# Squares of x summed on VectorE for one product, positions loaded between x's pieces, and GpSimd taken out of MLA and RWKV

## The chip, the cores and the metric

The kernel runs on one core of a Trainium2 chip. The metric is the device time of one execution in microseconds (us). Before the change the median of 3 runs is 1454.68 us (1453.99 to 1456.4).

A core has engines with an instruction queue each, worked off in order: TensorE (PE, matrix products), VectorE (DVE), ScalarE (ACT), GpSimd (POOL) and SyncE (SP), which here only issues transfers. An instruction waits at the head of its queue until what it needs has been signalled; everything behind it on that engine waits too.

## The reference

Two transformer blocks work on 256 tokens of 1024 numbers, in float32. The parts that matter here:

```python
def rms_norm(x, g):
    xf = x.astype(jnp.float32)
    y = xf * lax.rsqrt(jnp.mean(xf * xf, axis=-1, keepdims=True) + EPS)
    return (y * g.astype(jnp.float32)).astype(x.dtype)

h = x                                              # first block
u = rms_norm(h, g_mix) @ w_in                      # then rope on q, k; attention, cross attention, MLP
...
p = rms_norm_2(x, g_mix) @ w_in                    # second block
y_a = mla_group(p[..., :MLA_COLS], positions, ...) # attention with q, k normed per head and rotated in part
y_b = rwkv7_group(p[..., MLA_COLS:], ...)          # p + (prev - p) * mu, then a recurrence in chunks of 64
x = x + jnp.concatenate([y_a, y_b], axis=-1) @ w_o
x = x + peer_ffn(rms_norm_2(x, g_ffn), w_pq, ...)  # top-k choice of experts
```

In `mla_group` scores are scaled by the norms of query and key before the softmax. In `rwkv7_group` the keys are scaled by `a` and by a decay, and the output is normed per head.

## The kernel before

Activations lie transposed, channels on the 128 partitions and the 256 tokens along the row. A weight slab (128x1024 float32) is loaded, ScalarE rounds it to a high part (`hi`, L330), VectorE subtracts to get the low part (`lo`, L332), and three products (high by high, high by low, low by high) give a result near float32: L351, L352 and L354 in `lin` matmuls. A 128x256 matmul of them starts 0.12 us after the one before. The results stand in four banks called `lin`.

The program is written as Python generators and loops, and a scheduler fixes the order of each engine's queue when the program is built, from its own estimate of the times. What is told here of order is thus a consequence of the code and not written in it.

The stages in time: 0 to 72 us the start (load x, its mean square, the tables of the rotation, first slabs); to 436 us the rest of the first block; to 660 us the second block's `w_in2`, MLA and RWKV, and the output product `w_o`; to 800 us the choice of experts; to the end the experts themselves.

**Start.** x comes in five pieces (L252). For each of its eight 128x256 parts, `sumsq` (L504) squares it, on ScalarE or (every second one) GpSimd, and a product with `ones` on TensorE (L513) adds it up in `lin_139`: eight products. `act_split` (L356) makes the high and low part of x (`xsh`, `xsl`, L364). `rsq` (L488) turns the sum into `rb`, the inverse root, with two refining steps on VectorE. `trig` (L562 on) makes sines and cosines of the positions, one table on VectorE and one on GpSimd. The first seven slabs go through the `lin` matmuls without the norm, and evacuating a bank multiplies by `rb` (L635).

**Block 2, 436 to 660 us.** `ev2` (L992) evacuates a part of `w_in2`: product with the norm into `pr`, difference to the token before on GpSimd (L1016), and back on VectorE (L1018). `lo_engines` with `LO2S = 'VVVVG'` sends every fifth low part to GpSimd. RWKV runs in two generators `r0` and `r1` of four heads each, MLA in a third one. In RWKV GpSimd multiplies `kk` and `kp` by the decay `Ls` (L1091, L1098) and scales by `ln_w` (L1194). In MLA, `rotate` (L1451) lets GpSimd multiply and add (L1455, L1456); `scale_keys` (L1371) calls `rsq` in its light form, with two products on GpSimd (L500); `scores` (L1381) takes the row maximum (L1390), scales it (L1391), and the exponential and its sum follow; L1399 scales the result `me` and TensorE transposes it (L1405). `outputs` (L1410) forms one pair of heads: `myo` on VectorE, then its high part `y2h` on ScalarE (L660).

The end of an RWKV generator, as far as it matters: TensorE adds the last products into `w` (L1292, L1298); ScalarE squares (L1309), VectorE multiplies (L1310), TensorE sums per head (L1315), ScalarE takes the inverse root (L490, L491), VectorE finishes (L1317, L1318), ScalarE takes the high part `y2h` (L1319) and VectorE the low part (L1320). `lo2` multiplies all eight parts of `y2` by `w_o`.

The residual h was written out ("spill") since its place is used for RWKV's matrices. It is read back in four transfers (L1540, in the order 0, 2, 1, 3), each of which waits for the last reader of the matrices in its place: transfer 0 for r0's first matrices, transfer 2 for the ones that L1298 of r0 reads, 1 and 3 for r1's. GpSimd multiplies each by `r4` (L1541).

Of the kernel before, what the change touches and what calls it, by code (L numbers as in the profile page):

```python
# [9 lines left out]
F32 = mybir.dt.float32  # L10
# [10 lines left out]
P = 128  # L21
# [39 lines left out]
LIGHT = True  # L61
# [5 lines left out]
LO2S = 'VVVVG'  # L67
# [148 lines left out]
def body(tc, A, out):  # L216
# [3 lines left out]
    with es:  # L220
# [28 lines left out]
        for j0, j1 in ((0, 1), (1, 2), (2, 4), (4, 6), (6, 8)):  # L249
            if j0 == X_W:  # L250
                ahead = [load(A["w_in_s"][FIRST[0]])]
            nc.sync.dma_start(xt[:, j0:j1], A["xT"][:, j0:j1])  # L252
            if j0 == 0:
                nc.sync.dma_start(pv, A["pv"])
        if X_W > 6:
            ahead = [load(A["w_in_s"][FIRST[0]])]
# [19 lines left out]
        cst = early.tile([P, CL["inv"][0] - CB], F32, name="cst")  # L276
        nc.sync.dma_start(ident, A["consts"][:, :P])
        pi = st.tile([P, 2, T], I32, name="posi")
        for j in range(2):
            nc.sync.dma_start(pi[:, j], bass.AP(tensor=A["pos"].tensor, offset=A["pos"].offset + j * T, ap=[[0, P], [1, T]]))  # L280
        inv = const.tile([P, 4], F32, name="inv")
        nc.sync.dma_start(inv, A["consts"][:, CL["inv"][0]:])
# [205 lines left out]
        def rsq(dst, ss, n, eps=EPS, newton=None, tag="n", light=False, am=None):  # L488
# [3 lines left out]
            if newton is not None or am is not None:  # L492
                if am is None:
                    am = newton.tile(list(dst.shape), F32, tag=tag + "a", name=nm("am"), bufs=1)
                if light:
                    S.activation(am, ss, AF.Identity, scale=-0.5 / n, bias=NEPS[:dst.shape[0]])
                else:
                    V.tensor_scalar(am, ss, -0.5 / n, -0.5 * eps, op0=OP.mult, op1=OP.add)
                for _ in range(2):
                    (G if light else V).tensor_tensor(am, am, dst, op=OP.mult)  # L500
                V.scalar_tensor_tensor(dst, am, 1.5, dst, op0=OP.add, op1=OP.mult)
            return ins
# [140 lines left out]
        for j, (g, f) in enumerate((("g_qn", 96.0 ** -0.5), ("g_kn", 1.0))):  # L643
            G.tensor_scalar(tabs[:, 2 * j], mc[:, 0], pvc(g), f, op0=OP.mult, op1=OP.mult)
            G.tensor_scalar(tabs[:, 1 + 2 * j], mc[:, 1], pvc(g), f, op0=OP.mult, op1=OP.mult)
# [345 lines left out]

        def ev2(nb, ps):  # L992
            if nb < 5:
                c = ml.tile([P, T], F32, tag="prd", name=nm("cq"))
                V.tensor_tensor(c, ps, r5, op=OP.mult)
                i, dst, g = (nb, cqp, "g_cq") if nb < 3 else (nb - 3, ckp, "g_ckv")
                act_split(dst, c, i, pvc(g, i))
                i = nb // 3
                ssk[i].add(c)
                if nb == 2:  # L1000

                    p_ = ssk[0].col()
                    for i in range(2):
                        V.tensor_scalar(ecol[:, 2 * i:2 * i + 2], p_[:, 0:2], EPS / 384, EPS * EPS, op0=OP.mult, op1=OP.add)
                    ssk[1] = SumSq(ml, 2)
                elif nb == 4:
                    rsq(rk2, ssk[1].ps(True)[:, :T], 256, newton=ml, tag="n96")
            elif nb == 5:
                V.tensor_tensor(kro[64:], ps[64:], r5[64:], op=OP.mult)
            else:  # L1010
                b = nb - 6
                pr = ml.tile([P, T + 1], F32, tag="pr", name=nm("pr"))
                G.memset(pr[:, 0:1], 0.0)
                V.tensor_tensor(pr[:, 1:], ps, r5, op=OP.mult)
# [32 lines left out]
        def rwkv(g):  # L1047
# [43 lines left out]
            G.tensor_tensor(kk, kk, Ls, op=OP.mult)  # L1091
# [6 lines left out]
            G.tensor_tensor(kp, kp, Ls, op=OP.mult)  # L1098
# [224 lines left out]
        def mla():  # L1323
# [103 lines left out]
            def project(j):  # L1427
# [19 lines left out]
                S.activation(kgu[0:64], ksq[0:64], AF.Copy, scale=pvc("g_kn")[0:64])  # L1447
# [3 lines left out]
            def rotate(qf, qg):  # L1451
# [3 lines left out]
                G.tensor_tensor(qg, qf, b2(tabs[:, 0]), op=OP.mult)  # L1455
                G.tensor_tensor(qg[rr], qg[rr], t2[rr], op=OP.add)  # L1456
# [24 lines left out]
        lo_engines[:] = [{"V": V, "G": G}[c] for c in LO2S]  # L1481
# [53 lines left out]
        RESE = G  # L1535
# [275 lines left out]
```

## Time and profile before

| | us |
|---|---|
| median of the runs | 1454.68 |
| profiled execution | 1457.07 |
| span of its trace | 1455.3 |
| TensorE busy | 1421.4 (98%) |
| VectorE busy | 1061.5 (73%) |
| ScalarE busy | 767.3 (53%) |
| GpSimd busy | 148.1 (10%) |

The shares are means over the whole span. The end is set where TensorE waits, and a table by stretch shows where that is: a wait of the bounding engine counts, and idle time of another one costs nothing. The clock column is the granted share of TensorE's full speed.

### The profile page before, as it was taken

What the parts mean: (1) busy time and instruction counts of PE and PEld (TensorE: products, weight loads), DVE (VectorE), ACT (ScalarE), POOL (GpSimd) and SP (SyncE); (2) the same over time, 40 slices, a digit from 0 to 9 for tenths busy, and PEclk for the clock granted to TensorE, in tenths of its full rate; (3) what the DMA queues carried; (4) which work ended last, traced back from release to release, by engine and by line L of the source; (5) the groups of instructions that cost most, each with busy time, mean ns of one, the idle gap of its engine ahead of it and who ended that gap; (6) DMA issues with size and microseconds to landing.
All of it is one profiled execution on the core that took longest, in us unless ns stands there. A gap on an engine that the chain in (4) does not pass through costs nothing.

```text
span 1455.3 us, 25592 instructions
## 1 busy us (share of the span) xinstructions
PE 1421.4 (98%) x9950; PEld 1287.5 (88%) x9950; DVE 1061.5 (73%) x1900; ACT 767.3 (53%) x1248; POOL 148.1 (10%) x159
## 2 busy tenths in 40 slices
PE   8999999999999988999999999999999999999998
PEld 7888999888898867899999999999998888888887
DVE  7876676886659988579999778788875555555554
ACT  6856655555557445554445444444445454454443
POOL 6500101000115443220000000000000000000000
PEclk9999999999999998999999999999999999999999
DMA  6543445566665411155555555555455555555554
GB/s 209 175 156 102 144 144 154 183 190 201 198 191 156 135 44 37 33 162 186 159 187 176 178 171 160 164 159 170 149 174 186 190 200 189 193 198 189 197 193 145
DMA packets 75914, 237.43 MB, mean 163 GB/s; under 512 B 14608, under 2 KB 17808, under 8 KB 75792
## 3 DMA queue, kind: packets, MB, share of 16 engines
q1 hardware_dynamic: 75792, 235.79, 50.9%
q8 instruction: 78, 1.28, 0.4%
q14 instruction: 44, 0.36, 0.1%
HBM read 233.27 MB, written 2.49 MB: 162 GB/s over the span
## 4 chain that ended last, share of the span: by engine, by line
PE 90%; DVE 6%; DMA 2%; ACT 1%; issue 1%; SPq 0%; POOL 0%; DVEq 0%; ACTq 0%
PE lin L354 17%; PE lin L351 13%; PE lin L352 13%; PE lin L348 8%; PE w L1788 8%; PE w L1787 8%; PE w L1791 8%; PE w L1709 2%; DVE lo L332 1%; PE lin L484 1%; PE lin L485 1%; PE lin L486 1%; DMA raw<-w_pq 1%; PE w L1623 0%; PE lin L513 0%
## 5 line engine op out<-in xcount | busy, mean ns | idle before, releaser
L332 DVE TENSOR_TENSOR lo<-raw,hi 128x1024 fp32r<-128x1024 f32 (+1 forms) x432 | 531.7, 1232 | 275.7 <-PE w L1788 97.2
L330 ACT ACTIVATE hi<-raw 128x1024 fp32r<-128x1024 f32 x437 | 459.0, 1050 | 467.8 <-DMA raw<-eu 99.2
L351 PE MATMUL lin<-hbh,hi 128*128 128x256 f32 x1024 | 253.0, 284 | 0.0
L352 PE MATMUL lin<-hbl,hi 128*128 128x256 f32 x1024 | 252.3, 284 | 0.0
L351 PEld LDWEIGHTS lin<-hbh,hi 128*128 128x128 f32 x1024 | 196.1, 192 | 0.1
L352 PEld LDWEIGHTS lin<-hbl,hi 128*128 128x128 f32 x1024 | 196.2, 192 | 0.0
L1788 PE MATMUL w<-lo,wh 128*128 128x512 f32 x504 | 155.6, 390 | 0.0
L1791 PE MATMUL w<-hi,wl 128*128 128x512 f32 x504 | 155.2, 389 | 0.0
L354 PE MATMUL lin<-hbh,lo 128*128 128x256 f32 x1024 | 145.0, 284 | 0.7 <-DVE lo L332 0.7
L1787 PE MATMUL w<-hi,wh 128*128 128x512 f32 x504 | 134.8, 389 | 0.0
L354 PEld LDWEIGHTS lin<-hbh,lo 128*128 128x128 f32 x1024 | 132.1, 192 | 1.1 <-DVE lo L332 1.1
L1791 PEld LDWEIGHTS w<-hi,wl 128*128 128x128 f32 x504 | 94.6, 188 | 19.7
L1787 PEld LDWEIGHTS w<-hi,wh 128*128 128x128 f32 x504 | 94.6, 188 | 19.6
L1788 PEld LDWEIGHTS w<-lo,wh 128*128 128x128 f32 x504 | 94.3, 188 | 19.5
L1770 ACT ACTIVATE wh<-GA 128x512 fp32r<-128x512 f32 x64 | 40.5, 634 | 73.2 <-PE w L1788 73.2
L530 POOL TENSOR_TENSOR sqa<-sqa,sq 128x256 f32<-128x256 f32 x37 | 34.7, 937 | 315.3 <-ACT sq L526 300.3
L348 PE MATMUL lin<-a,hi 128*128 128x512 f32 x256 | 64.8, 395 | 0.0
L348 PE MATMUL lin<-xs,hi 128*128 128x512 f32 x256 | 63.3, 392 | 0.0
L348 PEld LDWEIGHTS lin<-xs,hi 128*128 128x128 f32 x256 | 46.4, 189 | 8.5
L354 PE MATMUL lin<-xs,lo 128*128 128x256 f32 x384 | 53.8, 285 | 0.0
L348 PEld LDWEIGHTS lin<-a,hi 128*128 128x128 f32 x256 | 45.9, 188 | 8.5
L354 PEld LDWEIGHTS lin<-xs,lo 128*128 128x128 f32 x384 | 50.9, 191 | 2.2
(582 smaller groups left out, 2583.8 us busy)
## 6 DMA issues: line engine op xcount, KB each, us to landing
raw<-eu SPq DMA_DIRECT2D x128, 512.0 KB, 3.6
raw<-ev SPq DMA_DIRECT2D x128, 512.0 KB, 3.4
raw<-w_up SPq DMA_DIRECT2D x32, 512.0 KB, 3.6
raw<-w_down SPq DMA_DIRECT2D x32, 512.0 KB, 4.5
raw<-w_in SPq DMA_DIRECT2D x20, 512.0 KB, 3.6
raw<-w_in_s SPq DMA_DIRECT2D x16, 512.0 KB, 4.8
raw<-w_pq SPq DMA_DIRECT2D x16, 512.0 KB, 3.5
raw<-w_in_m SPq DMA_DIRECT2D x8, 512.0 KB, 3.5
```

What stands on the lines that cost most here:

```text
L330: S.activation(hi[:, :n], raw[:, :n], AF.Copy)
L332: eng.tensor_tensor(lo[:, :n], raw[:, :n], hi.bitcast(F32)[:, :n], op=OP.subtract)
L348: PE.matmul(ps.rearrange("p (a t) -> p a t", a=2), lhsT=wh[:, o], rhs=x.both[:, c], start=at, stop=False, skip_group_check=True)
L351: PE.matmul(ps[:, :T], lhsT=wh[:, o], rhs=x[0][:, c], start=at, stop=False, skip_group_check=True)
L352: PE.matmul(ps[:, :T], lhsT=wh[:, o], rhs=x[1][:, c], start=False, stop=False, skip_group_check=True)
L354: PE.matmul(ps[:, :T], lhsT=wl[:, o], rhs=x[0][:, c], start=False, stop=stop and c == ks[-1][0], skip_group_check=True)
L530: G.tensor_tensor(self.acc, self.acc, q, op=OP.add)
L1709: PE.matmul(p_[:, o_:o_ + P], lhsT=first[:, i], rhs=parts[s][:, i], start=i % 4 == 0 and s == 0, stop=i % 4 == 3 and s == 1, skip_group_ch ...
L1770: S.activation(wh_, w2, AF.Copy)
L1787: PE.matmul(acc[t][d], lhsT=wh_[:, i, ts], rhs=vh[:, ds], start=c + i == 0, stop=False, skip_group_check=True)
L1788: PE.matmul(acc[t][d], lhsT=wh_[:, i, ts], rhs=vl[:, ds], start=False, stop=False, skip_group_check=True)
L1791: PE.matmul(acc[t][d], lhsT=wl_[:, i, ts], rhs=vh[:, ds], start=False, stop=False, skip_group_check=True)
```

## The change

The diff, cut to its core. What is left out of it are the removed constants and the places where they were passed.

```diff
+        def load_pos(j):
+            nc.sync.dma_start(pi[:, j], ...)
         for j0, j1 in ((0, 1), (1, 2), (2, 4), (4, 6), (6, 8)):
             nc.sync.dma_start(xt[:, j0:j1], A["xT"][:, j0:j1])
             if j0 == 0:
                 nc.sync.dma_start(pv, A["pv"])
+            elif j0 == 1:
+                load_pos(0)
+                nc.sync.dma_start(inv, A["consts"][:, CL["inv"][0]:])
...
+            if am is not None:
+                S.activation(am, dst, AF.Square, scale=(0.5 / n) ** 0.5)
+                V.scalar_tensor_tensor(am, ss, n * eps, am, op0=OP.add, op1=OP.mult)
+                V.scalar_tensor_tensor(dst, am, 1.5, dst, op0=OP.subtract, op1=OP.mult)
...
+        acc = st.tile([P, T], F32, tag="na", name="acc", bufs=1)
         for j in range(KC):
-            sumsq(st, xt[:, j], j, KC, ssp, bufs=4, pool_engine=j % 2 == 1)
+            q = acc if j == 0 else st.tile([P, T], F32, tag="sq0", name=nm("sq"), bufs=4)
+            if j % 2:
+                G.tensor_tensor(q, xt[:, j], xt[:, j], op=OP.mult)
+            else:
+                S.activation(q, xt[:, j], AF.Square)
+            if j:
+                V.tensor_tensor(acc, acc, q, op=OP.add)
             act_split(xs, xt[:, j], j, pvc("g_mix", j))
+        PE.matmul(ssp[:, :T], lhsT=ones, rhs=acc, start=True, stop=True)
...
-                G.memset(pr[:, 0:1], 0.0)
+                V.memset(pr[:, 0:1], 0.0)
-                G.tensor_tensor(d, pr[:, :T], pr[:, 1:], op=OP.subtract)
+                S.activation(d, pr[:, 1:], AF.Copy, scale=omm[:, b:b + 1])
-                V.scalar_tensor_tensor(dst, d, pvc("mu", b), pr[:, 1:], op0=OP.mult, op1=OP.add)
+                V.scalar_tensor_tensor(dst, pr[:, :T], pvc("mu", b), d, op0=OP.mult, op1=OP.add)
...
-            G.tensor_tensor(kk, kk, Ls, op=OP.mult)
+            V.tensor_tensor(kk, kk, Ls, op=OP.mult)
-            G.tensor_tensor(kp, kp, Ls, op=OP.mult)
+            V.tensor_tensor(kp, kp, Ls, op=OP.mult)
...
-                G.tensor_scalar(gt[g][:, i], gt[g][:, i], pvc("ln_w", j), None, op0=OP.mult)
+                S.activation(gt[g][:, i], gt[g][:, i], AF.Copy, scale=pvc("ln_w", j))
...
-                    V.tensor_tensor(sm[:, q:q + 1], sm[:, q:q + 1], r[:, 2 * i + q:2 * i + q + 1], op=OP.mult)
+                V.tensor_tensor(sm[:, 0:2], sm[:, 0:2], r[:, 2 * i:2 * i + 2], op=OP.mult)
...
-                G.tensor_tensor(qg, qf, b2(tabs[:, 0]), op=OP.mult)
-                G.tensor_tensor(qg[rr], qg[rr], t2[rr], op=OP.add)
+                S.activation(qg[0:64], qf[0:64], AF.Copy, scale=tabs[0:64, 0, 0:1])
+                V.tensor_tensor(qg[rr], qf[rr], b2(tabs[rr, 0]), op=OP.mult)
+                V.tensor_tensor(qg[rr], qg[rr], t2[rr], op=OP.add)
...
-        lo_engines[:] = [{"V": V, "G": G}[c] for c in LO2S]
...
-            RESE.tensor_tensor(xt[:, 2 * j:2 * j + 2], xt[:, 2 * j:2 * j + 2], r4[:, None].to_broadcast([P, 2, T]), op=OP.mult)
+            V.tensor_tensor(xt[:, 2 * j:2 * j + 2], xt[:, 2 * j:2 * j + 2], r4[:, None].to_broadcast([P, 2, T]), op=OP.mult)
```

So the eight squares are added on VectorE and one product makes the sum; the positions' first row and the frequencies are loaded behind x's second part; the light form of `rsq` becomes one square on ScalarE and two steps on VectorE, and gives the negative root, for which `g_kn` carries a minus; the interpolation with `mu` takes a precomputed `1 - mu`; the products with `Ls`, the rotation, all low parts and the residual's product run on VectorE, three scalings on ScalarE. In the changed file `rsq` stands at L490 on, the new sum at L607 and L609, its product at L613, the residual at L1557.

The scheduler's order at the places that the prediction speaks of. TensorE at the start of the program, before: `lin_139` collects the squares, `lin_255` is the first slab.

```order
L513 MATMUL lin_139<-sq_140,ones 128x256
L513 MATMUL lin_139<-sq_145,ones 128x256
L513 MATMUL lin_139<-sq_150,ones 128x256
L513 MATMUL lin_139<-sq_155,ones 128x256
L513 MATMUL lin_139<-sq_160,ones 128x256
L513 MATMUL lin_139<-sq_165,ones 128x256
L351 MATMUL lin_255<-xsh_131,hi_170 128x256
L352 MATMUL lin_255<-xsl_135,hi_170 128x256
```

TensorE at the start of the program, now:

```order
L613 MATMUL lin_139<-acc,ones 128x256
L353 MATMUL lin_255<-xsh_131,hi_169 128x256
L354 MATMUL lin_255<-xsl_135,hi_169 128x256
L353 MATMUL lin_255<-xsh_131,hi_169 128x256
L354 MATMUL lin_255<-xsl_135,hi_169 128x256
```

The one product stands ahead of every slab's matmul, and it needs all eight squares. The last sums on VectorE, now (`lo_171` and `lo_284` are the low parts of the first two slabs, `trig` and `tabs` the table of the rotation):

```order
L334 TENSOR_TENSOR lo_171<-raw_105,hi_169 128x1024
L609 TENSOR_TENSOR acc<-acc,sq_164 128x256
L366 SCALAR_TENSOR_TENSOR xsl_138<-h,pv,xsh_134 128x256
L583 SCALAR_TENSOR_TENSOR trig_194<-trig_193,trig_194 128x256
L366 SCALAR_TENSOR_TENSOR xsl_138<-h,pv,xsh_134 128x256
L609 TENSOR_TENSOR acc<-acc,sq_173 128x256
L334 TENSOR_TENSOR lo_284<-raw_110,hi_282 128x1024
L588 TENSOR_SCALAR tabs_129<-trig_194 128x256
L577 TENSOR_SCALAR trig_193<-trig_192 128x256
L609 TENSOR_TENSOR acc<-acc,sq_178 128x256
```

The sums stand among the low parts and the table's steps; before there were none. VectorE at the end of block 2, before, with what each row waits for (`w_6505` and `p_4976` are r0's, `w_6740` and `p_4990` r1's; `myo_6930` is the last pair of heads):

```order
L1424 SCALAR_TENSOR_TENSOR myo_6930<-lin_6919,pv,mr_6927 128x256 [waits Activation_49]
L1276 TENSOR_TENSOR h<-w_6634,lend_5770 128x128 [waits PE_49]
L1278 TENSOR_TENSOR h<-w_6634,cst 128x128
L1310 TENSOR_TENSOR p_4976<-w_6505,gt_4898 128x2x2x128 [waits Activation_49]
L661 TENSOR_TENSOR y2l_5810<-myo_6930,y2h_5808 128x256 [waits Activation_49]
```

The same place now (L1557 is the residual's product behind transfers 0 and 2, DMAHW the signal of a transfer; `p_4977` is r0's, `p_4991` r1's):

```order
L1301 TENSOR_TENSOR h<-w_6632,lend_5771 128x128 [waits PE_49]
L1557 TENSOR_TENSOR h<-h,r_4867 128x512 [waits DMAHW0_49]
L1301 TENSOR_TENSOR h<-w_6631,lend_5771 128x128 [waits PE_49]
L1557 TENSOR_TENSOR h<-h,r_4867 128x512 [waits DMAHW1_49,DVE_49]
L1441 SCALAR_TENSOR_TENSOR myo_6923<-lin_6912,pv,mr_6920 128x256 [waits Activation_49]
L672 TENSOR_TENSOR y2l_5811<-myo_6923,y2h_5809 128x256 [waits Activation_49]
L1326 TENSOR_TENSOR p_4977<-w_6504,gt_4899 128x2x2x128 [waits Activation_49]
L1326 TENSOR_TENSOR p_4991<-w_6737,wag 128x256 [waits Activation_49]
```

Two waits for transfers stand ahead of `myo` on VectorE. TensorE there, now (L1314 is what L1298 was; `lin_6927` and `lin_6976` are `w_o`'s first results, `w_6580` r0's sums per head):

```order
L1314 MATMUL w_6504<-kr_5256,h 64x64
L1314 MATMUL w_6737<-kr_5768,h 64x64
L353 MATMUL lin_6927<-y2h_5808,hi_6930 128x256
L354 MATMUL lin_6927<-y2l_5810,hi_6930 128x256
L353 MATMUL lin_6976<-y2h_5808,hi_6979 128x256
L353 MATMUL lin_6927<-y2h_5809,hi_6930 128x256 [waits Activation_49]
L1331 MATMUL w_6580<-p_4977,cst 128x512 [waits Activation_49]
L353 MATMUL lin_6927<-y2h_6533,hi_6930 128x256 [waits Activation_49]
```

The rows between them are further lin matmuls and are left out here: nine stand between the last L1314 and the first row that waits, six more ahead of L1331. Before, r1's products L1292 and L1298 stood behind these lin matmuls; now all of them stand ahead, r0's and r1's alternating to the same end.

## Rows read from the trace of the kernel before

**Rows 1.** The page's busy line: busy us, share of the span, instructions.
```profile
PE 1421.4 (98%) x9950; PEld 1287.5 (88%) x9950; DVE 1061.5 (73%) x1900; ACT 767.3 (53%) x1248; POOL 148.1 (10%) x159
```

**Rows 2.** By stretch: length, busy of PE, PEld, DVE, ACT, POOL, granted clock, DMA share.
```profile
480.00:562.00 82.00, 67.43 (x508) 55.57 (x507) 73.99 (x161) 36.92 (x69) 33.68 (x26) 0.90 0.25 70
...
600.00:636.00 36.00, 35.90 (x444) 31.86 (x445) 20.49 (x47) 18.67 (x40) 5.28 (x4) 1.00 0.36 107
```

**Rows 3.** TensorE's waits, 480 to 565 us: total, times, longest.
```profile
PE lin L1405 <- DVE me L1399: 6.5, 1, 6.5
```

**Rows 4.** Timeline of VectorE: start, duration, engine, line, operation.
```profile
524.92 2.31 DVE L1367 SCALAR_TENSOR_TENSOR qsc<-qsc 128x4 f32<-128x4 f32 x1
...
573.16 0.15 DVE L1367 SCALAR_TENSOR_TENSOR qsc<-qsc 128x4 f32<-128x4 f32 x1
```

**Rows 5.** Timeline of GpSimd at the same time.
```profile
524.83 2.38 POOL L332 TENSOR_TENSOR lo<-raw,hi 128x1024 fp32r<-128x1024 f32 x1
```

**Rows 6.** Groups of VectorE by shape, 480 to 562 us: total, mean ns, idle before.
```profile
L332 DVE TENSOR_TENSOR lo<-raw,hi 128x1024 fp32r<-128x1024 f32 x9 | 12.7, 1409 | 1.8 <-PE lin L354 1.2 <-issue 0.5
...
L1097 DVE SCALAR_TENSOR_TENSOR h<-h,pv,p 128x256 f32<-128x256 f32 x4 | 4.4, 1131 | 0.0
...
L1172 DVE TENSOR_TENSOR p<-p,t 64x8 f32<-64x8 f32 x8 | 2.9, 417 | 0.0
...
L1367 DVE SCALAR_TENSOR_TENSOR qsc<-qsc 128x4 f32<-128x4 f32 x2 | 2.5, 1226 | 0.0
...
L1172 DVE TENSOR_TENSOR p<-p,t 64x512 f32<-64x512 f32 x2 | 2.2, 1076 | 0.0
...
L1167 DVE TENSOR_TENSOR p<-p 64x64 f32<-64x64 f32 x4 | 1.9, 512 | 0.0
...
L501 DVE SCALAR_TENSOR_TENSOR n<-n,n 128x512 f32<-128x512 f32 x2 | 1.3, 672 | 0.0
...
L1368 DVE SCALAR_TENSOR_TENSOR qsc<-qsc 128x4 f32<-128x4 f32 x2 | 1.3, 659 | 0.0
```

**Rows 7.** Timeline of VectorE at the start of the program.
```profile
4.11 1.24 DVE L364 SCALAR_TENSOR_TENSOR xsl<-h,pv,xsh 128x256 fp32r<-128x256 f32 x2 [0.45 <-ACT xsh L363]
...
8.78 0.88 DVE L364 SCALAR_TENSOR_TENSOR xsl<-h,pv,xsh 128x256 fp32r<-128x256 f32 x2 [1.22 <-ACT xsh L363]
...
16.30 0.51 DVE L581 SCALAR_TENSOR_TENSOR trig<-trig,trig 128x256 f32<-128x256 f32 x1
...
17.36 1.22 DVE L332 TENSOR_TENSOR lo<-raw,hi 128x1024 fp32r<-128x1024 f32 x1
...
19.04 0.41 DVE L500 TENSOR_TENSOR am<-am,rb 128x256 f32<-128x256 f32 x1
```

**Rows 8.** Timeline of TensorE at the start of the program.
```profile
5.11 5.22 PE L513 MATMUL lin<-sq,ones 128*128 128x256 f32 x10 [0.17 <-POOL sq L508]
10.33 0.39 PE L351 MATMUL lin<-xsh,hi 128*128 128x256 f32 x1
10.55 0.28 PE L352 MATMUL lin<-xsl,hi 128*128 128x256 f32 x1
10.67 0.28 PE L351 MATMUL lin<-xsh,hi 128*128 128x256 f32 x1
...
11.86 1.02 PE L513 MATMUL lin<-sq,ones 128*128 128x256 f32 x4
...
36.03 0.40 PE L484 MATMUL lin<-hi,xsh 128*128 128x512 f32 x1
```

**Rows 9.** TensorE's waits, 0 to 72 us: total, times, longest.
```profile
PE lin L351 <- ACT hi L330: 1.3, 1, 1.3
```

**Rows 10.** The reload of the residual (L1540): from issue to landing.
```profile
DMA to landing us min/median/max: 3.5/3.5/3.5
```

**Rows 11.** Timeline of ScalarE at the end of r0.
```profile
612.36 0.60 ACT L1309 ACTIVATE p<-w 128x512 f32<-128x512 f32 x1
...
618.02 0.63 ACT L1319 ACTIVATE y2h<-p 128x512 fp32r<-128x512 f32 x1 [1.73 <-DVE p L1318]
```

More of the change, by code (lines that the diff above doesn't have):

```diff
@@ L60 @@
 MLA_STEPS = 1
-LIGHT = True
 MLA_PRIO = 200
@@ L66 @@
 PRE1 = 0
-LO2S = 'VVVVG'
 R1_PRIO = 100
@@ L248, in body @@
         xt = keep.tile([P, KC, T], F32, name="h")
[L249 to L256, printed above, removed]
         x0p = es.enter_context(tc.tile_pool(name="x0p", bufs=1))
@@ L276, in body @@
         cst = early.tile([P, CL["inv"][0] - CB], F32, name="cst")
-        nc.sync.dma_start(ident, A["consts"][:, :P])
[L278 to L282, printed above, removed]
+        pi = st.tile([P, 2, T], I32, name="posi")
+        inv = const.tile([P, 4], F32, name="inv")
+        def load_pos(j):
+            nc.sync.dma_start(pi[:, j], bass.AP(tensor=A["pos"].tensor, offset=A["pos"].offset + j * T, ap=[[0, P], [1, T]]))
+        for j0, j1 in ((0, 1), (1, 2), (2, 4), (4, 6), (6, 8)):
+            if j0 == X_W:
+                ahead = [load(A["w_in_s"][FIRST[0]])]
+            nc.sync.dma_start(xt[:, j0:j1], A["xT"][:, j0:j1])
+            if j0 == 0:
+                nc.sync.dma_start(pv, A["pv"])
+            elif j0 == 1:
+                load_pos(0)
+                nc.sync.dma_start(inv, A["consts"][:, CL["inv"][0]:])
+        nc.sync.dma_start(ident, A["consts"][:, :P])
+        load_pos(1)
         ahead.append(load(A["w_in_s"][FIRST[1]]))
@@ L486, in tok3, with rsq @@
             PE.matmul(ps, lhsT=xl, rhs=wh, start=False, stop=stop)
-        def rsq(dst, ss, n, eps=EPS, newton=None, tag="n", light=False, am=None):
+        def rsq(dst, ss, n, eps=EPS, newton=None, tag="n", am=None):
             S.activation(dst, ss, AF.Ln, scale=1.0 / n, bias=EPSB[eps][:dst.shape[0]] if eps else 0.0)
             ins = S.activation(dst, dst, AF.Exp, scale=-0.5)
[L492 to L498, printed above, removed]
+            if am is not None:
+                S.activation(am, dst, AF.Square, scale=(0.5 / n) ** 0.5)
+                V.scalar_tensor_tensor(am, ss, n * eps, am, op0=OP.add, op1=OP.mult)
+                V.scalar_tensor_tensor(dst, am, 1.5, dst, op0=OP.subtract, op1=OP.mult)
+            elif newton is not None:
+                am = newton.tile(list(dst.shape), F32, tag=tag + "a", name=nm("am"), bufs=1)
+                V.tensor_scalar(am, ss, -0.5 / n, -0.5 * eps, op0=OP.mult, op1=OP.add)
                 for _ in range(2):
-                    (G if light else V).tensor_tensor(am, am, dst, op=OP.mult)
+                    V.tensor_tensor(am, am, dst, op=OP.mult)
                 V.scalar_tensor_tensor(dst, am, 1.5, dst, op0=OP.add, op1=OP.mult)
@@ L641, in body @@
         lin_T(xs, A["w_in_s"], KC, FIRST, ev1)
-        for j, (g, f) in enumerate((("g_qn", 96.0 ** -0.5), ("g_kn", 1.0))):
+        for j, (g, f) in enumerate((("g_qn", 96.0 ** -0.5), ("g_kn", -1.0))):
             G.tensor_scalar(tabs[:, 2 * j], mc[:, 0], pvc(g), f, op0=OP.mult, op1=OP.mult)
@@ L990, in body @@
         ecol = ml.tile([P, 4], F32, name="ecol", bufs=1)
+        omm = pv[:, PV_LAYOUT["g_mix"][0]:PV_LAYOUT["g_mix"][0] + 14]
+        assert PV_LAYOUT["g_cross"] == (PV_LAYOUT["g_mix"][1], PV_LAYOUT["g_mix"][0] + 16)
+        V.tensor_scalar(omm, pv[:, PV_LAYOUT["mu"][0]:PV_LAYOUT["mu"][1]], -1.0, 1.0, op0=OP.mult, op1=OP.add)
         def ev2(nb, ps):
@@ L1375, in scale_keys @@
                 r, am = (ml.tile([P, 512], F32, tag="n96" + n, name=nm("n96"), bufs=1) for n in "ab")
-                rsq(r, p_, 96, am=am, light=LIGHT)
+                rsq(r, p_, 96, am=am)
                 kg = two("kg", 2)
@@ L1390, in scores @@
                     V.tensor_reduce(sm[:, q:q + 1], s_[:, k0:k1], axis=AX.X, op=OP.max, negate=True)
-                    V.tensor_tensor(sm[:, q:q + 1], sm[:, q:q + 1], r[:, 2 * i + q:2 * i + q + 1], op=OP.mult)
+                V.tensor_tensor(sm[:, 0:2], sm[:, 0:2], r[:, 2 * i:2 * i + 2], op=OP.mult)
+                for q, (k0, k1) in enumerate(spans):
                     S.activation(e[:, k0:k1], s_[:, k0:k1], AF.Exp, scale=r[:, 2 * i + q:2 * i + q + 1], bias=sm[:, q:q + 1],
@@ L1446, in project @@
                 V.tensor_tensor(ksq[0:64], ps[0:64].rearrange("p (a t) -> p a t", a=2), b2(rk2[0:64]), op=OP.mult)
-                S.activation(kgu[0:64], ksq[0:64], AF.Copy, scale=pvc("g_kn")[0:64])
+                S.activation(kgu[0:64], ksq[0:64], AF.Copy, scale=tabs[0:64, 2, 0:1])
                 S.activation(ksq[0:64], ksq[0:64], AF.Square)
@@ L1532, in body @@
         s6.close()
-        RESE = G
         xs6 = xpair("xs6", 2)
```

## The prediction

> **What bounds the kernel now.** I read the busy line first [rows 1]: TensorE works 98% of the span, so only what starts a matmul earlier or later moves the end. The table by stretch comes next [rows 2]. The stretch 480 to 562 us is the exception: 67.43 us of matmul in 82 us, VectorE at 73.99, granted clock 0.90. There VectorE bounds the kernel, while 600 to 636 us is full (35.90 of 36). The longest of TensorE's waits in it is 6.5 us for the scaled scores `me` (L1405), VectorE's work [rows 3].
>
> Why is VectorE late there? A 128x4 multiplication on it takes 2.31 us beside a subtraction on GpSimd of 2.38 us, and 0.15 us elsewhere [rows 4, 5]. The groups of that stretch show how often [rows 6].
>
> **The change part by part.** The sum is made against the profiled execution, 1457.07 us (span 1455.3), which lies 2.39 above the median of 1454.68.
>
> *Block 2, 436 to 565 us.* What goes is the excess of VectorE's instructions beside GpSimd. Against the clean durations (1.22 for the 128x1024 subtraction and 0.44 for 128x256 with a scalar [rows 7], 0.67 for 512 columns as in L501 [rows 6], 0.15 for the smallest [rows 4], an estimated 0.2 for 64x64) the groups L332, L1097, L1172 (64x8), L1367, L1368, L1172 (64x512) and L1167 give 9 x 0.19 + 4 x 0.69 + 8 x 0.27 + 2 x 1.08 + 2 x 0.51 + 2 x 0.41 + 4 x 0.31 = 11.9 us [rows 6]. What comes onto VectorE in the same stretch: two of the five subtractions (2.4), three of the four products with `Ls` (3 x 0.67 = 2.0), one more step of the key norm for each of two head pairs (1.3), the product and the sum of the rotation for two pairs (4 x 0.67 = 2.7), less two or three small products (-0.4): 8.0. That leaves -3.9 for an engine that sets the pace. In the 44 us before, three more subtractions, a product with `Ls` and the zeroing of 14 single columns come (an estimated 5 us) and about as much excess goes, or more. TensorE is nearly full there, so I credit only what VectorE no longer drags into 480 us: 0 to 4.5 (an estimate from the same kinds of excess), taken 3.0. Together -6.9. ScalarE takes over the interpolation and three scalings; it has room here and holds nobody. TensorE's idle time bounds the gain: 82 - 67.4 = 14.6 us [rows 2], and some slow clock; if the added work fills what is freed it is 1. The 6.5 us wait stays in my reading: between the last `AB` and the first `me` the new order on VectorE has the rotation's sum, one more norm step and a key product that stood elsewhere, some 2 us against the excess lost there.
>
> The Trainium skill (SBUF — State Buffer, section "SBUF: two separate sides") calls the pair of ports that VectorE and GpSimd share an exclusive lock, held for a whole instruction, not a split of bandwidth. The trace agrees: 2.31 us beside 2.38 [rows 4, 5]. By that rule even a tiny instruction waits out a long one, and removing all overlap frees every such wait; that is the first rival's mechanism.
>
> *Start.* Before, the eight sums of squares and the first lin matmuls take turns on TensorE: first lin matmul at 10.33 us [rows 8]. Now one product of `acc` stands ahead of all of them, and `acc` is complete only behind 8 low parts of x, 7 sums, 10 steps of the rotation's table and 2 subtractions on VectorE: 8 x 0.44 + 7 x 0.41 + 10 x 0.51 or less + 2 x 1.22 = 13.9 us or less from 4.11 us [rows 7]: 18.0 at most without waits, later if the positions land late, since they now stand between. I take 17.5, and 18.1 for the first lin matmul behind a 0.5 us product. Seven slabs of 24 matmuls follow at 0.12 each [rows 8], 20.2 us, with an estimated 0.6 us of small ones between: done at 38.9, against 36.0 now [rows 8], where the waits that stand between now fall away. That is +2.9. The first ten pieces of L513 took 5.22 us, twice as long each as the four at 11.86 us (1.02) [rows 8]. If the first matmuls of the program again take double for 6 us, now lin matmuls pay it: +3.0 more, and I take it since these rows are the nearest. TensorE's later wait of 1.3 us for ScalarE [rows 9], which the later matmuls don't move, should take up -1.3. Start: +4.6, bounds 0 and +8.
>
> *End of block 2, about 610 us.* Now r0's and r1's last products L1298 end side by side (call this t0), and the scaling of the reloaded residual stands on VectorE, ahead of `myo`. The second reload can be issued only after r0's last L1298 and lands 3.5 us later [rows 10]; on GpSimd this wait harmed nobody. VectorE: landed at t0+3.5, product 0.67 (as L501), `myo` an estimated 0.5 (half the columns); ScalarE's `y2h` an estimated 0.4 (half the columns of L1309); with some overlap the tenth lin matmul starts at t0+5.0 to 5.2, where TensorE arrives at t0+1.1 (nine at 0.12): 4.1 us of wait. Behind `y2h` on ScalarE stand the squares L1309 (0.60 [rows 11]), so L1315 starts at t0+6.0 and ends at 7.3; then L490, L491, three steps on VectorE and `y2h` again. Before, from the end of L1309 (612.96) to the end of that `y2h` (618.65) took 5.7 us [rows 11], covered by r1's matmuls; no such cover is left. From t0+5.8, the end of L1309 now, it would reach t0+11.5 at most and 11.2 with matmuls waiting for it: TensorE idles 3.9 us from 7.3. The low part of `y2h` is late by 0.9 more. In sum +8.9, and 1.0 for a clock that falls after such waits, as the granted 0.90 of the stretch with the long wait shows [rows 2] (0 to 4): +9.9. If the reload landed at once the second and third waits would remain, less 0.5: +4.3. Low and high: +4 and +13.
>
> The Trainium skill (SBUF — State Buffer, section "The DMA setup-cost knee") gives a transfer about 2 us fixed plus its bytes at 436 GB/s; for 256 KB an estimate of 2.6 us, where the trace has 3.5 [rows 10]. By it the first wait would be 0.9 shorter and the total 0.9 less; the trace's figure is used.
>
> Sum: -6.9 + 4.6 + 9.9 = +7.6, so 1464.7 profiled, about 1462.3 as a median.
>
> **The rivals.**
> 1. Faster: the waits on VectorE were due to GpSimd wholly, and the freed engine runs ahead, so that the long wait halves as well (6.5 to 3 with half its slow clock): -12. The start costs +1.5 (positions early, no slow first matmuls) and the tail only +4.3. Total -6.2: 1448.5. For it: 11.9 us of excess sit where VectorE is the bound. Against: 8.0 us come back on the same engine, and the order leaves a long queue before `me`. It decides where VectorE's excess outweighs the added work by more than about 10 us.
> 2. No change: the scaling's wait is shorter since the reload goes out before r1's last products end (tail +4.3), the start is absorbed to +2.5: -6.9 + 4.3 + 2.5 = 0: 1454.7. For it: later stages have slack on VectorE and ScalarE. Against: both of r0's and r1's L1298 alternate to the same end.
> 3. The change doesn't relieve: long VectorE instructions have another cause, or its added work fills the gap: -1, with start and tail in full (+14.5): +13.5, 1468.2. Against: the pair 2.31 and 2.38 starts and ends together [rows 4, 5].
>
> **How the numbers follow.** The forecast has 0.50 with its own range +2 to +13 (1457 to 1468); rival 1 has 0.23, rival 2 0.15, rival 3 0.12. A difference under 0.2% (2.9 us) cannot be told from none. Slower by more: 0.43 of the forecast, all of rival 3, 0.02 of rival 2: 0.57. Faster: 0.19 of rival 1, 0.03 of rival 2 and 0.01 of the forecast: 0.23. Same: 0.20. The range 1449 to 1469 leaves out about one in ten at either end.
>
> **What would show it.** In the changed profile: first lin matmul at 17 to 19 us and no wait behind it; VectorE's 128x4 and 64x8 instructions back to 0.15 us, TensorE's waits in that stretch gone but for L1405; near 610 to 625 us two waits of TensorE of 3 to 5 us, the first for `y2h` behind the reload, the second for the normalized `y2h`. I am wrong if TensorE stays full from 600 to 636 us, if the first lin matmul starts before 13 us, or if VectorE's stretch 480 to 562 shrinks by more than 12 us.

## The result, and the profile after

The changed kernel takes 1464.61 us (median of 4 runs, 1463.57 to 1467.12); the kernel before, run beside it, 1455.54 (1453.99 to 1456.42, 4 runs). The ratio is 1.0059, 95% interval 1.0039 to 1.0078: slower, by 9.1 us of median. The profiled execution took 1465.07 us, 8.0 above that of before.

The page's busy line of the changed kernel answers to [rows 1]:

```profile
PE 1416.6 (97%) x9936; PEld 1286.7 (88%) x9936; DVE 1056.5 (72%) x1939; ACT 777.0 (53%) x1270; POOL 81.3 (6%) x98
```

TensorE is busy 4.8 us less in a span that is 7.9 us longer: the time went into waits. Where, is read best by following one matmul: its start in the changed kernel less the start of the same one (same source line, same tiles, same place in their sequence) in the kernel before. The median of this shift over a stretch of before's time, for the changed kernel and for the experiments below. The last column but one is read from TensorE's timeline: whether r0's last products (`w<-kr,h`) run well ahead of r1's, as in the kernel before, or end together with them.

| kernel | 400-436 us | 590-600 us | from 670 us | end of block 2 | median of runs |
|---|---|---|---|---|---|
| changed | +7.5 | +2.6 | +8.6 | together | 1464.61 |
| e1 old start | -1.3 | -0.9 | +4.2 | together | 1460.52 |
| e2 before, new start | +7.8 | +9.0 | +9.2 | r0 ahead | 1466.03 |
| e3 residual on GpSimd | +7.1 | +1.5 | +9.2 | together | 1465.35 |
| e4 before, low parts | -2.1 | -1.3 | +5.4 | together | 1463.20 |
| e6 late product | +8.0 | +1.9 | +9.3 | together | 1464.40 |
| e7 warm | +5.2 | +6.1 | +9.0 | r0 ahead | 1466.14 |
| e8 old start, rank | -0.4 | -4.5 | -1.3 | r0 ahead | 1452.59 |
| e9 rank | +6.0 | -3.3 | -1.3 | r0 ahead | 1459.93 |
| e11 old sum | +2.7 | -3.0 | -3.8 | r0 ahead | 1452.97 |
| e12 table later | +5.7 | -2.5 | +4.9 | together | 1463.17 |
| e13 before, rank | +2.0 | +5.7 | +9.9 | r0 ahead | 1461.56 |
| e14 table later, rank | +7.1 | -1.4 | +0.4 | r0 ahead | 1456.98 |

The changed kernel loses 7.5 us at the start, wins back 4.9 in block 2 and loses 6.0 at its end; behind 670 us nothing moves any more. The kernel before has a median of 1455.8 to 1456.2 in the sittings of the experiments. A shift comes from one execution; executions of one kernel differ by some us (before: 1451.9 to 1460.8), so differences under 2 us between rows are not read. The profiled execution lies within 2 us of its kernel's median but in three rows: e8 (2.6 above), e9 (4.9 below) and e13 (5.3 above). The column at 590 to 600 us is the softest, since matmuls change places where the order is another one: for the changed kernel it has +2.6, and the shift over 600 to 612 us is +4.0.

**Block 2.** By stretch (columns as in [rows 2]), the changed kernel; the first row is the stretch that holds the work of before's 480 to 562 us, by its matmuls (506 against 508):

```profile
489.00:566.00 77.00, 67.89 (x506) 58.16 (x505) 66.76 (x164) 38.65 (x74) 5.03 (x4) 0.84 0.28 77
...
600.00:636.00 36.00, 31.92 (x389) 26.07 (x389) 18.75 (x50) 15.64 (x37) 0.00 (x0) 0.95 0.16 46
```

The same matmuls take 77 us instead of 82, and VectorE 66.76 us instead of 73.99 [rows 2]. Its groups in this stretch (total, mean ns) answer to [rows 6]:

```profile
L334 DVE TENSOR_TENSOR lo<-raw,hi 128x1024 fp32r<-128x1024 f32 x11 | 13.4, 1218 | 3.1 <-issue 1.5 <-PE lin L343 1.3 <-PE lin L356 0.3
...
L1113 DVE SCALAR_TENSOR_TENSOR h<-h,pv,p 128x256 f32<-128x256 f32 x2 | 0.9, 471 | 0.0
...
L1183 DVE TENSOR_TENSOR p<-p 64x64 f32<-64x64 f32 x4 | 0.8, 247 | 0.0
...
L1188 DVE TENSOR_TENSOR p<-p,t 64x8 f32<-64x8 f32 x8 | 0.8, 151 | 0.0
```

1409 ns became 1218, 1131 became 471, 512 became 247 and 417 became 151: the excess beside GpSimd is gone. In the timeline of VectorE the 128x4 multiplication of 2.31 us [rows 4] is

```profile
561.52 0.14 DVE L1383 SCALAR_TENSOR_TENSOR qsc<-qsc 128x4 f32<-128x4 f32 x1
```

The Trainium skill (SBUF — State Buffer, section "SBUF: two separate sides"), by which the shared ports are held for a whole instruction, fits this: without a long GpSimd instruction beside it the small one takes 0.14. TensorE's waits in the changed kernel from 436 to 660 us (total, times, longest) show what remains:

```profile
PE lin L1422 <- DVE me L1416: 7.4, 2, 7.0
PE lin L353 <- DVE pr L1030: 2.6, 1, 2.6
PE lin L353 <- ACT y2h L1335: 2.6, 1, 2.6
...
PE w L1077 <- DMA lora<-lora: 1.0, 1, 1.0
...
PE w L1331 <- ACT p L492: 0.7, 1, 0.7
```

The long wait for `me` stays, 7.0 us for 6.5 [rows 3], as forecast.

### The profile page after: what moved, and what is told of

Same layout as the page of the kernel before. It is cut to its first block, busy times and chain, and to the rows that moved or that the text cites. A ratio compares the mean times of both kernels' runs of the same rounds, so it can differ in the third digit from the quotient of the medians.

```text
span 1463.2 us, 25535 instructions
## 1 busy us (share of the span) xinstructions
PE 1416.6 (97%) x9936; PEld 1286.7 (88%) x9936; DVE 1056.5 (72%) x1939; ACT 777.0 (53%) x1270; POOL 81.3 (6%) x98
## 4 chain that ended last, share of the span: by engine, by line
PE 90%; DVE 5%; ACT 2%; DMA 2%; issue 1%; POOL 0%; SPq 0%; DVEq 0%; ACTq 0%
PE lin L356 18%; PE lin L353 13%; PE lin L354 13%; PE lin L350 8%; PE w L1804 8%; PE w L1803 8%; PE w L1807 8%; PE w L1725 2%; DVE lo L334 1%; PE lin L486 1%; PE lin L487 1%; PE lin L488 1%; ACT hi L332 1%; PE w L1639 0%; ACT qraw L638 0%
## 5 line engine op out<-in xcount | busy, mean ns | idle before, releaser
L334 DVE TENSOR_TENSOR lo<-raw,hi 128x1024 fp32r<-128x1024 f32 x437 | 534.3, 1224 | 282.4 <-PE w L1804 94.0
L1807 PEld LDWEIGHTS w<-hi,wl 128*128 128x128 f32 x504 | 94.6, 188 | 19.7
```

Source lines behind the costliest of these rows:

```text
L334: eng.tensor_tensor(lo[:, :n], raw[:, :n], hi.bitcast(F32)[:, :n], op=OP.subtract)
L1807: PE.matmul(acc[t][d], lhsT=wl_[:, i, ts], rhs=vh[:, ds], start=False, stop=False, skip_group_check=True)
```

## The experiments

All against the kernel before on the same chip. "Changed" is the kernel after the change; its 1464.61 comes from the first sitting, and the kernel before, run in every sitting, differs by 0.7 us at most between them.

**e1: old start.** The changed kernel with eight products and the old order of loads.

```diff
-        (x's pieces with positions and frequencies among them; acc; one product)
+        (x's pieces first, positions behind the slabs)
+            sumsq(st, xt[:, j], j, KC, ssp, bufs=4, pool_engine=j % 2 == 1)
```

> The changed kernel with the old start alone: eight products for x's squares and the old order of loads. Theory: the start costs 7.3 us by itself and nothing later gives it back, so about 1457.3 us (7.3 under the changed kernel); the wait near 625 us for the normalized y2h stays. Rival: the late start is swallowed by VectorE's lateness around 450 to 550 us, so undoing it brings 3 us or less, 1461.5 or more.

Measured 1460.52, ratio 1.0030 (1.0015 to 1.0045), between the two expectations. The start's shift goes from +7.5 to -1.3, so the new start costs about that much; but of the 8.8 us only 4 reach the end, since block 2 as a whole no longer gains (-1.3 to -0.9). The scheduler had laid it out anew: the stretch in which VectorE sets the pace still gains (from +2.9 at 470 us to -5.5 at 560), but 4.2 us are lost ahead of it and 4.5 behind it.

**e2: new start alone,** on the kernel before (the diff of e1 the other way round).

> The kernel before with the new start alone (sums on VectorE, one product, positions among x's pieces). Theory: first lin matmul near 19 us at half pace until 24 us, about +7.3 us, so 1462.8 us, and no wait near 625 us. Rival: TensorE's waits at 480 to 565 us of the kernel before take up half of it, so 1459 us.

Measured 1466.03, ratio 1.0070 (1.0056 to 1.0085), 3.2 above the theory's time: +7.8 from the start, as the theory has it, and it stays and grows to +9.2 at the end. The start by itself costs more than the whole forecast. The parts don't add up: the start alone costs 10.2 us of median, all the rest alone (e1) 4.7, both together 9.1, since the order differs each time.

**e3: residual's product back on GpSimd,** in the changed kernel.

```diff
-            V.tensor_tensor(xt[:, 2 * j:2 * j + 2], ...
+            G.tensor_tensor(xt[:, 2 * j:2 * j + 2], ...
```

> The changed kernel with the residual's four products back on GpSimd. Theory: the alternation of r0 and r1 makes the loss near 625 us, not the product's wait on VectorE, so 0 to -0.5 us against the changed kernel (1464.2). Rival, the first term of the prediction's tail: the waits behind the reloaded residual cost about 4 us, so 1460.5 us.

Measured 1465.35, ratio 1.0058 (1.0043 to 1.0073): no change against the changed kernel. The reload ahead of `myo` on VectorE costs nothing.

**e4: all low parts on VectorE,** in the kernel before.

```diff
-LO2S = 'VVVVG'
+LO2S = 'VVVVV'
```

> The kernel before with every low part on VectorE (5 subtractions moved from GpSimd), nothing else. Its order has r0's and r1's last products alternate, as in the changed kernel. Theory: the tail loses 5.5 us by that order and block 2 gains 2 to 4, so about 1458 us, and VectorE's instructions of over 2 us are gone. Rival: the alternation costs nothing by itself, so 1452 us.

Measured 1463.20, ratio 1.0052 (1.0038 to 1.0067), slower than either expectation (the profiled execution is a low one, span 1460.7). The shift is -1.3 at 590 us and +5.4 behind 670. In this order, too, r0's and r1's last products alternate to one end, and TensorE's timeline has the wait behind it:

```profile
618.74 0.70 PE L1315 MATMUL w<-p,cst 128*128 128x256 f32 x2 [0.86 <-ACT p L490]
...
623.68 0.80 PE L351 MATMUL lin<-y2h,hi 128*128 128x256 f32 x2 [4.24 <-ACT y2h L1319]
```

So the loss at the end of block 2 needs no residual and no rotation on VectorE: the order alone brings it. VectorE's 128x4 multiplication that took 2.31 us beside GpSimd's subtraction [rows 4, 5] is down to 0.14 here, where the only edit took those subtractions off GpSimd:

```profile
522.33 0.14 DVE L1367 SCALAR_TENSOR_TENSOR qsc<-qsc 128x4 f32<-128x4 f32 x1
```

One instruction over 2 us is left on VectorE in block 2, a subtraction of 2.20, so the theory's "gone" holds but for that one.

**e6: the product behind the first two slabs,** in the changed kernel.

```diff
-        PE.matmul(ssp[:, :T], lhsT=ones, rhs=acc, ...)
+        for nb in FIRST[:2]:
+            lin_part(ps, xs, A["w_in_s"], KC, nb, 0, KC)
+        with tc.issue_after(lastmm[-1].ins):
+            PE.matmul(ssp[:, :T], lhsT=ones, rhs=acc, ...)
```

> The changed kernel, but the one product of the sum of squares stands on TensorE behind the 48 matmuls of the first two slabs instead of ahead of them. Theory (the start costs 7.3 us since every slab waits behind a product that is ready only at 18.5 us): the first lin matmul starts at 10 to 12 us, the matmuls between 72 and 440 us come 0 to 3 us later than in the kernel before instead of 7.3, and the median is about 1459 us. Rival (the start is late since the positions delay x's parts, or the slabs' low parts are late on VectorE): the shift stays at 5 us or more, and the median at 1462.5 or above.

Measured 1464.40, ratio 1.0052 (1.0038 to 1.0066). TensorE's timeline:

```profile
10.82 0.58 PE L355 MATMUL lin<-xsh,hi 128*128 128x256 f32 x1 [10.82 <-ACT hi L332]
...
19.26 0.59 PE L621 MATMUL lin<-acc,ones 128*128 128x256 f32 x2
...
30.67 0.36 PE L355 MATMUL lin<-xsh,hi 128*128 128x256 f32 x1 [2.43 <-DVE qk L653]
...
51.21 0.79 PE L489 MATMUL lin<-lo,xsh 128*128 128x512 f32 x1 [3.17 <-DVE lo L334]
```

The first lin matmul starts at 10.82 as meant, and the time doesn't move: the banks are still emptied late, behind the same late sum (2.43), and at 51 us a low part is not ready (3.17). The theory falls in this form: moving the product's place on TensorE gains nothing. The waits point to the late sum and to VectorE's queue instead; e11 and e12 try those.

**e12: the rotation's table behind the last sum,** in the changed kernel.

```diff
+        with tc.issue_after(lastadd.ins):
             trig(V, 0, tabs1[:, 0], tabs1[:, 1])
```

> The changed kernel, but the rotation's table on VectorE is issued only behind the last sum, so that only x's low parts and one low part of a slab stand among the seven sums. Theory (sums late behind other work of VectorE): acc is complete at 12 to 13.5 us instead of 18.5, the first lin matmul starts at 13 to 14, the matmuls between 72 and 440 us come 1 to 4 us late instead of 7.3, and the median is 1458 to 1461. Rival (the start is bound by the chain from the sum over the inverse root to the slabs' evacuation, or by the weights' rounding, whatever the sum's time): the shift stays at 6 or more, and the median at 1463 or above.

Measured 1463.17, ratio 1.0049 (1.0036 to 1.0062). TensorE's timeline:

```profile
14.27 1.22 PE L613 MATMUL lin<-acc,ones 128*128 128x256 f32 x2 [14.27 <-DVE acc L609]
14.93 0.78 PE L353 MATMUL lin<-xsh,hi 128*128 128x256 f32 x1
...
53.33 0.79 PE L487 MATMUL lin<-lo,xsh 128*128 128x512 f32 x1 [2.80 <-DVE lo L334]
```

The product starts 4.2 us earlier (18.51 in the changed kernel), though later than the theory's 12 to 13.5, and the shift at 400 to 436 us falls by 1.8 only, nearer to the rival: 2.8 us go at 53 us, in a wait for a low part that was 0.4 in the changed kernel. The next bound of the start lies right behind the sum, on VectorE.

**e11: eight products again, new order of loads kept,** in the changed kernel (the sums' part of e1's diff).

> The changed kernel with the eight products for the sum of squares back on TensorE, while positions and frequencies stay loaded among x's pieces. Theory (the start's 7.3 us come from the sums, which stand behind the rotation's table and two low parts on VectorE, and not from x's later landing): the first lin matmul starts before 12 us, the matmuls between 72 and 440 us come -1 to +2 us against the kernel before, median 1456 to 1460 us. Rival (the order of the loads): a shift of 4 us or more there, and 1461 or above.

Measured 1452.97, ratio 0.9979 (0.9968 to 0.9991): 11.6 us below the changed kernel, faster than before and than either expectation. The start's shift is +2.7, between theory and rival. With e1 (-1.3) and the changed kernel (+7.5) it parts the start: about 4 us by the loads, about 5 by the sum. The loads' part isn't lost where x lands: the first lin matmul starts at 11.09, and from 30 to 48 us the matmuls come 1.0 early. It is lost behind that, in a wait for a low part and a granted clock of 0.80 from 48 to 52 us:

```profile
49.52 0.50 PE L487 MATMUL lin<-lo,xsh 128*128 128x512 f32 x1 [1.83 <-DVE lo L334]
```

The rest of the gain wasn't meant: without a word on it in the code, the scheduler now lets r0's last products run ahead of r1's. TensorE's waits from 436 to 660 us begin

```profile
PE lin L353 <- DVE pr L1022: 2.6, 1, 2.6
PE w L1206 <- DVE AB L1147: 1.9, 1, 1.9
PE w L1218 <- DMA p<-blk_out: 1.8, 1, 1.8
```

and neither the wait for `me` nor one for `y2h` is among them.

**e7: TensorE kept busy ahead of the product,** in the changed kernel.

```diff
+            for _ in range(50):
+                PE.matmul(wm[:, :P], lhsT=ones, rhs=ones, start=True, stop=True)
```

> The changed kernel with 50 added products of ones with ones (128x128, results unused) on TensorE ahead of the one product, from about 1 us to about 17 us. Theory (the first lin matmuls take 0.21 us each instead of 0.12, up to 24.2 us, because TensorE did nothing ahead of them): they now start 0.12 us apart from the first, the shift against the kernel before falls from 7.3 to about 4.8 us, and the median is about 1462.3. Rival (the pitch of 0.21 comes from what they read or wait for, such as low parts and weights): the pitch stays, and the median at 1464.6 or above.

Measured 1466.14, ratio 1.0063 (1.0046 to 1.0080). TensorE's timeline, and below it the stretch 19.7 to 23 us:

```profile
1.05 13.75 PE L604 MATMUL w<-ones 128*128 128x128 f32 x100 [1.05 <-DVE ones L307]
18.18 0.70 PE L618 MATMUL lin<-acc,ones 128*128 128x256 f32 x2 [3.38 <-DVE acc L614]
...
18.96 0.28 PE L354 MATMUL lin<-xsh,hi 128*128 128x256 f32 x1
19.08 0.28 PE L355 MATMUL lin<-xsl,hi 128*128 128x256 f32 x1
...
20.16 0.42 PE L354 MATMUL lin<-xsh,hi 128*128 128x256 f32 x1
20.37 0.41 PE L355 MATMUL lin<-xsl,hi 128*128 128x256 f32 x1
```

```profile
19.70:23.00 3.30, 3.30 (x18) 3.30 (x17) 2.94 (x8) 3.17 (x5) 3.05 (x4) 0.50 0.09 35
```

The added products ended at 14.80, and 3.38 us of idle time followed. The first lin matmuls start 0.12 us apart, as the theory said, then 0.21 at a granted clock of 0.50. So the pace hangs on what TensorE did before; the shift fell to 5.2, near the 4.8 expected. The median didn't follow: in block 2 this order gains nothing (+5.2 to +6.1), though the wait for `me` is only 1.1 us in it; others stand in its place (4.0 for `AB`, 2.6 for `hi`, 2.3 for `p`).

**e8: old start, residual on GpSimd and a higher rank for r0,** in the changed kernel (e1's and e3's diffs and the line below).

```diff
-R0_PRIO = 100
+R0_PRIO = 150
```

> The changed kernel with the old start (eight products, old order of loads), the residual's product back on GpSimd, and a higher rank for r0 in the scheduler (R0_PRIO 150 instead of 100), so that r0's last products stand well ahead of r1's again and 19 matmuls of w_o stand between them. Theory (the tail's loss is the lost cover: both generators ending at the same time): no wait over 1.5 us between 612 and 632 us, and the median is 1453 to 1456, 4.5 to 7.5 us below the changed kernel with the old start alone (1460.5). Rival (the tail loses by other work moved onto VectorE and ScalarE): 1459 or above.

Measured 1452.59, ratio 0.9972 (0.9962 to 0.9983): faster than both kernels and, with e11, the best version here, by 3.6 us against before and 12 against the changed kernel; a little better than the theory's 1453 to 1456. From 612 to 632 us one wait over 0.3 us is left, 1.58 us for ScalarE's `hi`, where the theory had none over 1.5. With the cover back, the two waits for r0's and r1's ends are gone. Against e1 it differs in the rank and in the residual's place, and e3 finds no effect of the latter.

**e9: the rank alone,** in the changed kernel.

> The changed kernel with a higher rank for r0 alone (R0_PRIO 150 instead of 100): r0's last products stand ahead of r1's, and six matmuls of w_o stand behind them and ahead of r1's last. Theory (the tail's 5.5 us are the lost cover): the waits of 0.7 and 2.6 us at 624 to 628 us go or halve, and the median is 1460 to 1462, 3 to 4.5 below the changed kernel. Rival (other work): 1464 or above.

Measured 1459.93, ratio 1.0030 (1.0020 to 1.0041): 4.7 below the changed kernel, just past the theory's 3 to 4.5. Of the waits at the tail one of 0.9 for a low part is left. Its runs spread from 1455.1 to 1465.4 and the profiled one is the lowest, so its shifts are some 5 us too good.

**e13: the rank alone, in the kernel before.**

> The kernel before with the higher rank for r0 alone (R0_PRIO 150). Theory (the changed kernel with the old start and this rank gains 3.6 us, 1452.6, since VectorE is relieved of GpSimd in block 2; the rank only gives back the cover at the tail, which the kernel before has anyway): 1454 to 1459, no gain. Rival (the rank is the gain): 1453 or below.

Measured 1461.56, ratio 1.0038 (1.0022 to 1.0055): the rival falls, and the theory is 2.6 us short; the rank by itself does harm. Its runs spread from 1457.1 to 1466.9 and the profiled one is the highest, so its shifts are some 5 us too bad. TensorE's longest wait in its block 2 is that of before:

```profile
PE lin L1405 <- DVE me L1399: 6.5, 1, 6.5
```

The gain of e8 thus isn't the rank's alone: it needs the change of block 2 with it.

**e14: table behind the sums, and the rank,** in the changed kernel.

> Both repairs together in the changed kernel: table behind the sums, and R0_PRIO 150. Theory (two separate losses, start and tail, that add up): 1453.5 to 1457. Rival (one eats the other, as when the start's gain is lost again by waits in block 2): 1459 or above.

Measured 1456.98, ratio 1.0006 (0.9997 to 1.0016), inside the theory's numbers, and 7.6 below the changed kernel, where the two repairs alone brought 1.4 (e12) and 4.7 (e9). That the two losses add up is not shown by it, though: at 400 to 436 us the shift is still +7.1, with a wait of 2.8 us for the low part at 53 us as in e12, so the start's loss is not repaired. The gain stands in block 2 (+7.1 to -1.4) and in its end, which costs 1.8 us instead of 6.0. In this form the change is worth nothing against before.

## Why the prediction was right, and where its terms were off

The sign, the forecast case (+7.6; 8.0 between the profiled executions) and the three places were right. The terms were less so: each is off by 2 to 4 us, and their errors cancelled. That the sum came so close is luck.

**Start: forecast +4.6, measured +7.5.** VectorE's timeline in the changed kernel shows the last sums behind a slab's low part and the table's steps, as said:

```profile
15.69 0.51 DVE L609 TENSOR_TENSOR acc<-acc,sq 128x256 f32<-128x256 f32 x1
16.12 1.41 DVE L334 TENSOR_TENSOR lo<-raw,hi 128x1024 fp32r<-128x1024 f32 x1
17.46 0.37 DVE L588 TENSOR_SCALAR tabs<-trig 128x256 f32<-128x256 f32 x1
17.75 0.38 DVE L577 TENSOR_SCALAR trig<-trig 128x256 f32<-128x256 f32 x1
18.05 0.41 DVE L609 TENSOR_TENSOR acc<-acc,sq 128x256 f32<-128x256 f32 x1
```

and TensorE's:

```profile
18.51 1.22 PE L613 MATMUL lin<-acc,ones 128*128 128x256 f32 x2 [18.51 <-DVE acc L609]
19.17 0.78 PE L353 MATMUL lin<-xsh,hi 128*128 128x256 f32 x1
19.75 0.41 PE L354 MATMUL lin<-xsl,hi 128*128 128x256 f32 x1
19.96 0.41 PE L353 MATMUL lin<-xsh,hi 128*128 128x256 f32 x1
...
24.17 0.28 PE L353 MATMUL lin<-xsh,hi 128*128 128x256 f32 x1
24.29 0.28 PE L354 MATMUL lin<-xsl,hi 128*128 128x256 f32 x1
```

The first lin matmul came at 19.17, not 18.1 (+1.1), just outside the 17 to 19 named as a sign. The double price of the first matmuls held: 5.0 us from 19.17 to 24.17 for 24 that take 2.9 elsewhere, 2.1 instead of 3.0. The step that failed is the -1.3 from the wait for ScalarE [rows 9]: two waits for `hi` of 0.40 and 0.83 still stand at 53 and 54 us, and 0.82 for `lo` and `sq` came beside them. That is 4.6 + 1.1 - 0.9 + 1.2 + 0.8 = 6.8 of 7.5. Named only as a risk ("later if the positions land late"), and not priced, was the order of the loads: e11 puts about half of the loss there, though not where the risk was seen.

**Block 2: forecast -6.9, measured -4.9.** VectorE's ledger was too low: its busy time in the stretch fell by 7.2 us, not 3.9. Of these TensorE got 5.0; the wait for `me` kept its length and the clock fell to 0.84. The step that failed is the -3.0 credited for the 44 us ahead, which was wrong in sign: at 470 to 480 us the shift had grown by 1.2, with the wait for `pr` at 2.6 (1.7 before) and one of 1.0 for a transfer.

**End of block 2: forecast +9.9, measured +6.0.** The first of the two waits, 4.1 us, didn't come. The step that failed is "the second reload can be issued only after r0's last L1298". The queue of SP, the end of r1's L1299, and VectorE:

```profile
612.20 0.33 SPq L1556 DMA_DIRECT2D h<-spill  x1
616.01 0.33 SPq L1556 DMA_DIRECT2D h<-spill  x1
620.09 0.80 SPq L1556 DMA_DIRECT2D h<-spill  x2
```

```profile
615.57 0.40 PE L1299 MATMUL w<-h 64*64 64x64 f32 x7
```

```profile
618.96 0.69 DVE L1557 TENSOR_TENSOR h<-h,r 128x512 f32<-128x512 f32 x1 [2.65 <-DMA h<-spill]
619.57 0.48 DVE L1441 SCALAR_TENSOR_TENSOR myo<-lin,pv,mr 128x256 f32<-128x256 f32 x1
```

The second reload goes out at 616.01, right behind r1's L1299 and 4 us ahead of the end of the last L1314: it waits for r1's first matrices and not for r0's last, since the order of the transfers had changed too. The code has 0, 2, 1, 3, but the scheduler's queue of SP in the changed kernel has 0, 1, 2, 3, and the second one waits for L1299 of r1. So the second L1557 in the order of VectorE shown ahead of the prediction stands behind transfer 1, and not 2 as said there. `y2h` was ready at 620.50, and TensorE passed its tenth matmul, at about 621.2, without a wait. The second wait came, behind the shorter one for L1331, as TensorE's timeline and the stretch of slow clock behind it show:

```profile
618.78 1.38 PE L1314 MATMUL w<-kr,h 64*64 64x64 f32 x38
...
624.26 0.70 PE L1331 MATMUL w<-p,cst 128*128 128x256 f32 x2 [0.71 <-ACT p L492]
627.54 0.68 PE L353 MATMUL lin<-y2h,hi 128*128 128x256 f32 x2 [2.58 <-ACT y2h L1335]
628.61 0.58 PE L354 MATMUL lin<-y2l,hi 128*128 128x256 f32 x1 [0.39 <-DVE y2l L1336]
```

```profile
627.69:631.11 3.42, 3.03 (x13) 2.74 (x14) 1.71 (x5) 1.36 (x3) 0.00 (x0) 0.50 0.00 0
```

0.71 + 2.58 + 0.39 = 3.7 of the 4.8 forecast for this chain, and a slow clock behind it, about 1.5 us for 3.0 us of matmuls at 0.50 (1.0 forecast); 0.8 stays unexplained, less than the softness of the measured +6.0. That it is the lost cover, as said, is shown by the table, column "from 670" less column "590-600": where both generators end together this stretch costs +5.1 to +7.7 (changed, e1, e3, e4, e6, e12), and each of these six traces has a stretch of 3.4 to 6.8 us at a granted clock of 0.50 between 620 and 635 us. Where r0 runs ahead it costs -0.8 to +3.2 (e2, e7, e8, e9, e11, e14), and no clock falls there. The rank alone (e9), which changes only the order, leaves one wait of 0.9 us where 0.7 and 2.6 stood. e13, where r0 runs ahead as well and no clock falls, has +4.2 in its slowest execution, spread over short waits, and isn't explained.

Rival 1 (the freed engine halves the long wait) was wrong for this kernel. Its mechanism comes true in e11, where the wait for `me` is gone; but a short wait is not enough, as e7 shows, where it is 1.1 us and block 2 gains nothing. Rival 3 (another cause) is ruled out by the durations, by e4's 0.14 us and by the shorter stretch.

## What to carry to other kernels

Replacing eight small products by sums on another engine moves the work's place in that engine's queue: price the last of the sums with everything that stands ahead of it, and then the next bound behind it, here a low part at 50 us. Where a scheduler lays out the order, an edit at the start can re-order the end: look first whether two chains that covered each other now end together. A freed engine pays only if the order uses it: the same change is 0.6% slower, or 0.2 to 0.3% faster with the old sum (e11) or with the old start, the residual on GpSimd and a higher rank (e8).

## What the runs showed of the hardware

The slow pace of the first matmuls (0.21 us apart instead of 0.12) stands under a clock column of 1.00, in the changed kernel from 18 to 24 us:

```profile
18.00:24.00 6.00, 5.49 (x25) 5.31 (x26) 5.82 (x18) 4.06 (x7) 5.51 (x6) 1.00 0.29 89
```

Later in a program the same pace stands under 0.50, behind the wait at 627 us:

```profile
628.50:631.00 2.50, 2.39 (x11) 2.39 (x12) 0.79 (x4) 0.84 (x1) 0.00 (x0) 0.50 0.00 0
```

So it is the lower of the two levels of the clock, by its pace, and e7 bears that out: with TensorE busy ahead, the same matmuls start 0.12 us apart. At the start of a program the column doesn't tell of it. The clock's records in the changed kernel's trace begin only at 23.54 us, with 1.00, and ahead of the first record the column reads 1.00 as well; in e11 they begin at 12.89 us, where its first lin matmuls go from 0.21 to 0.12 apart. At the start, read the pitch and not the column.
